# Routing rebuilt: the sample's tile first, each tile routed by itself behind the next tile's product

## The chip, the core and the metric

The kernel runs on one core of a Trainium2 chip. A core has a matrix engine (PE, with its weight loads PEld), three engines for elementwise work (DVE, ACT, POOL), and SP, which here issues DMAs. Each engine works through its own instructions in order, and semaphores order the engines against each other. The metric is the device time of one execution in microseconds.

## What is computed

One layer of a streaming encoder for 512 prompt tokens and 64 sample tokens of 1024 features, all in float32: adaLN modulation, one input projection, sparse attention beside a convolution branch, a gated merge, an output projection, a residual with LayerNorm, and a mixture of 16 experts in 4 groups. The part that matters here is the last one:

```python
x = layer_norm(ALPHA * x + (1 + gate_1) * (merged @ w_o))      # 512 + 64 rows
h = x * (1 + scale_2) + shift_2
gl = h @ w_group + b_group                  # 4 groups: the largest logit
rl = h @ w_router + b_router                # 4 x 4 experts: the two largest of the group
y = sum over the two experts of weight * (silu(h @ gate) * (h @ up)) @ down
x = layer_norm(ALPHA * x + (1 + gate_2) * y)
```

## The kernel before

Tokens lie in five tiles: t = 0..3 are the prompt's, 128 rows each, and t = 4 is the sample's, 64 rows. The **output projection** runs in two halves of 512 columns. In the first half five PSUM banks (`o0` to `o4`) are filled side by side. In the second half (`o1`, from two banks that are used in turn) the tiles follow each other: 24 matmuls for a prompt tile (three for each of 8 feature tiles, since values and weights are split into two parts, hi and lo), 16 for the sample's. After a tile's product DVE adds the residual (`residual`: `rt`, then `xn`), takes the row statistics (`bs`, `mv`), ACT the square root and the normalisation (`xn` in place), PE turns the normalised rows (`ph`, 8 transposes), ACT copies them (`h2T`), and PE multiplies them with the router's 20 columns (`prt`, 8 matmuls). `h2_rows` scales the rows and adds them to `h_scr` in DRAM, `ax_rows` does the same for the result's residual share (`z_scr`); of the five multiplications of `ax_rows`, DVE has two and POOL three.

**Routing** (`route`) runs in two batches, tiles 0 to 2 and tiles 3 and 4, when their logits are there: about 30 small DVE instructions a batch find the group, the two experts and their one-hot rows (`Ej`), PE counts the rows ahead of each (`prank`), DVE builds one-hot ranks (`ohr`), and PE turns them into lists of token numbers (`pid`). From these come `idt`, the rows that POOL gathers from `h_scr` for an expert (`xg`), and the weights (`pwt`, `wsl`). `table` writes slots and weights to DRAM with ten indirect DMAs (`ids_scr`), from which two small lists (`ido`, then `so`) are read back for second blocks of experts.

**Experts.** The first four are fixed, the others follow in the order of their number of rows. Unit by unit, weights come through a ring of 24 pieces, are split into hi (ACT) and lo (DVE), and PE multiplies: gathered rows turned (`pxt`), `pg` in four steps of six matmuls, `hm` (silu on ACT, product on DVE), turned again (`pht`, which in the program stands behind the next unit's first two steps), `pd`, and a scatter to `z_scr`. The list of PE, DVE and ACT from there on is written out by hand (`manual_schedule`). Up to there a scheduler orders the instructions of each engine. The weights of experts 0 to 2 and 3 are loaded ahead of it.

A few lines carry the steps (`G` is POOL, `V` DVE, `S` ACT):

```python
    (G if t > 1 else V).tensor_tensor(xn[t][0:n], xn[t][0:n], axr[0:n], op=OP.mult)
...
    route(0, 3)
    h2_rows(3)
    route(3, NT)
    h2_rows(4)
```

## Time and profile before

| | us |
|---|---|
| device time, median of 3 runs | 880.16 (871.29 to 882.45) |
| span of the profiled execution | 874.9 |
| PE busy | 786.5 (90%) |
| DVE busy | 637.2 (73%) |
| ACT busy | 357.5 (41%) |
| POOL busy | 148.5 (17%) |

The profiled execution lasted 874.9 us from its first to its last instruction; a time of its own is not given, and the median of the runs is 5.3 us above this span. Busy shares are means over the whole span. In the rows below, a row of the timeline is start, duration, engine, line, operation, output from input, shapes, how many instructions in a row are counted together, and in brackets how long the engine was idle before and what ended that.

### The profile page before, as it was taken

The page shows a single profiled execution, that of the slowest core. Times are in us where ns is not written, and L with a number is a line of the kernel's source. Part 1 is how long each engine was busy: PE and PEld are TensorE (multiplying, and loading weights), DVE is VectorE, ACT ScalarE, POOL GpSimd, SP SyncE. Part 2 cuts the span into 40 slices and gives each one's busy share as a digit, 9 for nine tenths or more (in the row PEclk, how much of TensorE's full clock was granted, in tenths as well). Part 3 has the DMA queues.
Part 4 walks back from the last instruction along what each step waited for, and adds up shares of the span by engine and source line. Part 5 has one row for each costly group of instructions (what it writes and reads, how often), then busy time and mean ns, then how long its engine had stood idle before and what let it go on. Part 6 is the DMA issues. An engine that isn't in the chain of part 4 may idle for free. (4 is left out here: it accounts for less than half of the span.)

```text
span 874.9 us, 13257 instructions
## 1 busy us (share of the span) xinstructions
PE 786.5 (90%) x4827; PEld 637.9 (73%) x4827; DVE 637.2 (73%) x1256; ACT 357.5 (41%) x647; POOL 148.5 (17%) x180
## 2 busy tenths in 40 slices
PE   4899999999999999999999999999946999999900
PEld 3788888887878879879899789988835676556200
DVE  1569999989999889988878434628795886674323
ACT  3243232324344335547743852322433664354213
POOL 2300000310100000000010001020348332322213
PEclk9999999999999999999999999999957999999965
DMA  9997664572523224232474205785897998799446
GB/s 291 341 350 248 210 199 128 116 252 56 148 73 93 80 75 115 89 100 65 133 204 130 61 1 184 244 273 193 174 309 203 335 367 290 204 359 348 113 121 110
DMA packets 109329, 161.53 MB, mean 185 GB/s; under 512 B 9730, under 2 KB 67226, under 8 KB 109264
## 3 DMA queue, kind: packets, MB, share of 16 engines
q1 hardware_dynamic: 93664, 117.49, 41.6%
q0 software_dynamic: 14000, 38.98, 17.9%
q10 hardware_dynamic: 1600, 4.22, 1.3%
q8 instruction: 38, 0.62, 0.3%
q14 instruction: 27, 0.22, 0.1%
HBM read 145.49 MB, written 28.49 MB: 199 GB/s over the span
## 5 line engine op out<-in xcount | busy, mean ns | idle before, releaser
L588 DVE SCALAR_TENSOR_TENSOR y<-ue,dwT,y 128x604 f32<-128x604 f32 (+17 forms) x232 | 183.5, 829 | 1.9 <-ACT y L586 1.5
L242 PE MATMUL acc<-hh,wlo 128*128 128x288 f32 (+1 forms) x504 | 152.8, 304 | 1.5 <-DVE wlo L140 1.5
L243 PE MATMUL acc<-hh,whi 128*128 128x288 f32 (+1 forms) x504 | 150.4, 299 | 0.0
L244 PE MATMUL acc<-hl,whi 128*128 128x288 f32 (+1 forms) x504 | 149.4, 300 | 0.0
L139 ACT CAST whi<-wraw 128x1024 fp32r<-128x1024 f32 (+1 forms) x72 | 75.0, 1043 | 170.7 <-PE acc L244 75.0
L140 DVE TENSOR_TENSOR wlo<-wraw,whi 128x1024 fp32r<-128x1024 f32 (+1 forms) x72 | 87.4, 1214 | 52.1 <-ACT whi L139 51.9
L242 PEld LDWEIGHTS acc<-hh,wlo 128*128 128x128 f32 (+1 forms) x504 | 94.2, 187 | 17.4 <-issue 8.8
L243 PEld LDWEIGHTS acc<-hh,whi 128*128 128x128 f32 (+1 forms) x504 | 94.3, 187 | 5.2 <-issue 5.1
L244 PEld LDWEIGHTS acc<-hl,whi 128*128 128x128 f32 (+1 forms) x504 | 93.7, 187 | 5.5 <-issue 5.2
L144 PE MATMUL tm<-wlo,hh 128*128 128x512 f32 x128 | 50.5, 397 | 0.4 <-DVE wlo L140 0.4
L145 PE MATMUL tm<-whi,hh 128*128 128x512 f32 x128 | 50.4, 394 | 0.0
L146 PE MATMUL tm<-whi,hl 128*128 128x512 f32 x128 | 49.8, 392 | 0.0
L140 DVE TENSOR_TENSOR wlo<-ring,whi 128x1024 fp32r<-128x1024 f32 x30 | 36.3, 1222 | 14.9 <-ACT whi L139 9.5
L1179 PE MATMUL pd<-ring,hT 128*128 128x512 f32 x96 | 43.7, 598 | 0.5 <-issue 0.5
L139 ACT CAST whi<-ring 128x1024 fp32r<-128x1024 f32 x30 | 31.3, 1050 | 28.6 <-PE pg L146 19.3
L242 PE MATMUL acc<-oh,wlo 128*128 128x288 f32 x128 | 39.1, 306 | 1.7 <-DVE gt L748 1.4
L244 PE MATMUL acc<-yl,whi 128*128 128x288 f32 x128 | 39.1, 308 | 0.6 <-DVE yl L725 0.5
L1194 POOL DMA_INDIRECT z_scr<-yo,idt x16 | 27.2, 1702 | 69.3 <-DVE yo L1190 19.4
L242 PE MATMUL acc<-yh,wlo 128*128 128x288 f32 x128 | 38.9, 305 | 0.0
L244 PE MATMUL acc<-ol,whi 128*128 128x288 f32 x128 | 38.1, 300 | 0.0
L243 PE MATMUL acc<-yh,whi 128*128 128x288 f32 x128 | 37.9, 298 | 0.0
L714 POOL DMA_DIRECT2D gates_scr<-glg x16 | 8.7, 542 | 171.9 <-ACT glg L713 93.1
(479 smaller groups left out, 1792.9 us busy)
## 6 DMA issues: line engine op xcount, KB each, us to landing
ring<-in_w_gate_up_dram SPq DMA_DIRECT2D x62, 512.0 KB
wraw<-in_w_in_dram SPq DMA_DIRECT2D x48, 512.0 KB
wada<-in_w_ada_dram SPq DMA_DIRECT2D x32, 512.0 KB
ring<-in_w_down_dram SPq DMA_DIRECT2D x32, 512.0 KB
wada<-in_w_ada_dram SPq DMA_DIRECT2D x32, 256.0 KB
gates_scr<-glg POOLq DMA_DIRECT2D x16, 288.0 KB
gt<-gates_scr POOLq DMA_DIRECT2D x16, 288.0 KB
wraw<-in_w_conv_out_dram SPq DMA_DIRECT2D x8, 512.0 KB
```

Of the source, the lines that this page charges most:

```text
L139: split_copy[0] = S.copy(hi, raw).ins
L140: V.tensor_tensor(lo, raw, hi, op=OP.subtract)
L144: PE.matmul(out, lh, rl, start=start, stop=False)
L145: PE.matmul(out, lh, rh, start=False, stop=False)
L146: PE.matmul(out, ll, rh, start=False, stop=stop)
L242: PE.matmul(ps[h][0:m, 0:288], wl[:, k, :], xh[:, k, sl], start=k == 0, stop=False)
L243: PE.matmul(ps[h][0:m, 0:288], wh[:, k, :], xh[:, k, sl], start=False, stop=False)
L244: return PE.matmul(ps[h][0:m, 0:288], wh[:, k, :], xl[:, k, sl], start=False, stop=k == KT - 1).ins
L588: V.scalar_tensor_tensor(y[:, 30 - i:EXT], ue[:, 0:EXT - 30 + i], dwT[:, j, i:i + 1], y[:, 30 - i:EXT], op0=OP.mult, op1=OP.add)
L714: G.dma_start(gates_d[m], sg)
L1179: PE.matmul(pd_[c], hT[:, k, :], dns[0][k][:, cs], start=k == 0, stop=k == 1)
L1194: sc = G.indirect_dma_start(out=z_d, out_offset=bass.IndirectOffsetOnAxis(ap=idx[0:128 // len(ids)], axis=0), in_=y[half], in_offset=None, ...
```

## The change

The order of the second half becomes `ORDER = [4, 0, 1, 2, 3]`. All of PE's, DVE's and ACT's instructions from there to the experts are now in the hand-written list. Behind each step of a tile's product stands one step of the tile before (`before`) : its residual and statistics, the turning, the router, the choice, the counts, the lists. The rows are turned and multiplied before they are normalised; the mean and the deviation are put right afterwards on the 24 logits (`swn`, `brs`). The router's eight matmuls stand in four strips of 32 columns of the array, and a ninth (`plog`) adds the strips. The choice uses DVE's instructions for the eight largest values and their places. POOL does no multiplication any more: DVE does all of `ax_rows`, the last two of them, the weights, the slots and `table` behind the second step of unit 0 (`behind_first`). Expert 2's weights are loaded ahead as before, expert 3's behind the gathered rows of block 0. ACT loads its tables for Exp and Silu in `weigh`, ahead of the gathered rows.

```diff
+ORDER = [4, 0, 1, 2, 3]
...
-    for t in range(NT):
+    for t in ORDER:
         residual(t, ps[t], 0)
+        half_stats(t, 0)
...
+        def turn(self, b):
+            t, n = self.t, self.n
+            if b == 0:
+                self.xT = wp.tile([128, KT, 128], F32, name="h2T", tag="wraw", bufs=2)
+            ph = trp("ph2")
+            for i in range(4):
+                k = 4 * b + i
+                PE.transpose(ph[:, 128 * i:128 * i + n], xn[t][0:n, 128 * k:128 * k + 128], ident[0:n, 0:n])
+            S.copy(self.xT[:, 4 * b:4 * b + 4, 0:n], ph.rearrange("p (k t) -> p k t", k=4)[:, :, 0:n])
+        def residual(self):
+            residual(self.t, self.po, 1)
+            half_stats(self.t, 1)
+            self.mean, self.rs = stats(None, self.n, bss[self.t])
+        def router(self, b):
+            n = self.n
+            if b == 0:
+                self.pr = dot("prt")
+            for j in range(4):
+                k = 4 * b + j
+                PE.matmul(self.pr[32 * j:32 * j + 32, 0:n], routers[self.s][:, k, :], self.xT[:, k, 0:n], start=b == 0, stop=b == 1,
+                          tile_position=(0, 32 * j))
+            if b == 1:
+                self.prs = late.tile([128, 128], F32, name="prs", tag="hm", bufs=3)
+                S.copy(self.prs[:, 0:n], self.pr[:, 0:n])
+        def logits(self):
+            n = self.n
+            self.pl = dot("plog")
+            PE.matmul(self.pl[0:n, 0:RE], self.prs[:, 0:n], strips[:, 0:RE], start=True, stop=True)
+        def normal(self):
+            n, t, x = self.n, self.t, xn[self.t]
+            if self.last:
+                h2 = self.h2 = h2s[self.p % 2]
+                V.scalar_tensor_tensor(h2[0:n], x[0:n], self.mean, GS[self.s][0:n], op0=OP.subtract, op1=OP.mult)
+                self.normed = S.activation(h2[0:n], h2[0:n], AF.Copy, scale=self.rs).ins
+                G.dma_start(dap(h2_d, t * 128 * D, [[D, n], [1, D]]), h2[0:n], accum_op=OP.add)
+                return
+            nm = late.tile([128, 1], F32, name="nm", tag="nm", bufs=2)
+            V.scalar_tensor_tensor(nm[0:n], self.mean, -1.0, self.rs, op0=OP.mult, op1=OP.mult)
+            S.activation(x[0:n], x[0:n], AF.Identity, bias=nm[0:n], scale=self.rs)
+        def h2_rows(self):
+            n, t = self.n, self.t
+            h2 = h2s[self.p % 2]
+            V.tensor_tensor(h2[0:n], xn[t][0:n], GS[self.s][0:n], op=OP.mult)
+            G.dma_start(dap(h2_d, t * 128 * D, [[D, n], [1, D]]), h2[0:n], accum_op=OP.add)
+        def ax_rows(self):
+            n, t, x = self.n, self.t, xn[self.t]
+            if self.last:
+                V.scalar_tensor_tensor(x[0:n], x[0:n], self.mean, axr[0:n], op0=OP.subtract, op1=OP.mult)
+                S.activation(x[0:n], x[0:n], AF.Copy, scale=self.rs)
+            else:
+                V.tensor_tensor(x[0:n], x[0:n], axr[0:n], op=OP.mult)
+            ax_sums.append(G.dma_start(dap(z_d, t * 128 * D, [[D, n], [1, D]]), x[0:n], accum_op=OP.add).ins)
+        def choose(self):
+            p, n, s = self.p, self.n, self.s
+            R = rlog[:, p, :]
+            V.scalar_tensor_tensor(R[0:n], swn[0:n, s, :], self.mean, self.pl[0:n, 0:RE], op0=OP.mult, op1=OP.add)
+            V.scalar_tensor_tensor(R[0:n], R[0:n], self.rs, brs[0:n, s, :], op0=OP.mult, op1=OP.add)
+            V.max(m8g[:, p, :], R[:, 0:RG])
+            V.max_index(i8g, m8g[:, p, :], R[:, 0:RG])
+            r16 = late.tile([128, 16], F32, name="r16", bufs=1)
+            V.tensor_tensor(r16, group16, i8g[:, 0:1].to_broadcast([128, 16]), op=OP.not_equal)
+            V.scalar_tensor_tensor(r16, r16, NEG, R[:, RG:RE], op0=OP.mult, op1=OP.add)
+            V.max(m8e[:, p, :], r16)
+            V.max_index(i8e[:, p, :], m8e[:, p, :], r16)
+            E = Ej[:, :, p, :]
+            V.tensor_tensor(E, iota16[:, None, :].to_broadcast([128, 2, 16]), bc(i8e[:, p, 0:2], 16), op=OP.is_equal)
+            V.tensor_tensor(mb[:, p, :], E[:, 0], E[:, 1], op=OP.add)
+            if s:
+                V.memset(mb[64:128, p, :], 0.0)
+        def places(self):
+            p = self.p
+            self.pk = dot("prank")
+            PE.matmul(self.pk[:, 0:16], tri, mb[:, p, :], start=True, stop=False)
+            PE.matmul(self.pk[:, 0:16], onesb, mp[:, p, :], start=False, stop=True)
+        def ranks(self):
+            p = self.p
+            if not ohr:
+                ohr.append(late.tile([128, 2, NT, 128], F32R, name="ohr", tag="ohr", bufs=1))
+            V.tensor_tensor(mp[:, p + 1, :], mp[:, p, :], mb[:, p, :], op=OP.add)
+            self.vid = late.tile([128, 2, 16], F32R, name="vid", tag="vid", bufs=2)
+            V.tensor_scalar(self.vid, Ej[:, :, p, :], tok1[:, p:p + 1], None, op0=OP.mult)
+            er = late.tile([128, 2, 16], F32, name="er", tag="er", bufs=1)
+            V.tensor_tensor(er, Ej[:, :, p, :], self.pk[:, None, 0:16].to_broadcast([128, 2, 16]), op=OP.mult)
+            V.tensor_reduce(rk[:, :, p], er, axis=AX.X, op=OP.add)
+            V.tensor_tensor(ohr[0][:, :, p, :], iota128[:, None, :].to_broadcast([128, 2, 128]), bc(rk[:, :, p], 128),
+                            op=OP.is_equal)
+        def tokens(self):
+            p, n = self.p, self.n
+            for j in range(2):
+                PE.matmul(pid[:, 0:16], ohr[0][0:n, j, p, :], self.vid[0:n, j, :], start=p == 0 and j == 0,
+                          stop=self.last and j == 1)
...
+    row, before, rowq = None, None, []
+    for p in range(NT):
+        before, row = row, Row(p)
+        rowq.append(row)
+        for k, _ in enumerate(row.product()):
+            if k == 0:
+                row.turn(0)
+                if before is not None:
+                    before.residual()
+            if k == 1:
+                row.router(0)
+            if before is None:
+                continue
+            if k == 2:
+                before.turn(1)
+                before.normal()
+            if k == 3:
+                before.router(1)
+                before.h2_rows()
+            if k == 4:
+                before.logits()
+                before.choose()
+            if k == 6:
+                before.places()
+                before.ranks()
+                if p < NT - 1:
+                    before.ax_rows()
+            if k == 7:
+                before.tokens()
+    row.residual()
+    row.turn(1)
+    row.normal()
+    row.router(1)
+    row.logits()
+    row.choose()
+    row.places()
+    row.ranks()
+    row.tokens()
...
+    def weigh():
+        V.tensor_tensor(gex, rlog[:, :, 0:4], bc(m8g[:, :, 0], 4), op=OP.subtract)
+        V.tensor_tensor(w12[:, :, 1], m8e[:, :, 1], m8e[:, :, 0], op=OP.subtract)
+        S.activation(gex, gex, AF.Exp)
+        S.activation(w12[:, :, 1], w12[:, :, 1], AF.Exp)
+        silu = late.tile([128, 1], F32, name="silu", bufs=1)
+        S.activation(silu, epst, AF.Silu)
...
+    with routing:
+        los = []
+        split_ahead(2, los)
+        weigh()
+        los.pop(0)()
+        with tc.issue_after(rows_in(0)):
+            load_first(3)
+        los.pop(0)()
+        split_ahead()
         pend, over = [], overflow()
+        def behind_first():
+            weights()
+            weight_columns()
+            room[True] = 1
+            slots()
+            for p in (NT - 2, NT - 1):
+                rowq[p].ax_rows()
+            gr0s.append(late.tile([128, D], F32, name="gr0", tag="row0", bufs=1))
+            brow(gr0s[0], rows_d, 4 * D)
+            table()
...
                 step(1, p, False)
+                if u == 0:
+                    behind_first()
```

Three places show what this does to the engines' lists. **PE, second half of the output projection.** Before, the second half begins with tile 0 (`o_6023`):

```order
L786 MATMUL pbr<-bw,ones 128x40
L144 MATMUL o_6023<-wo,mh 128x512
L145 MATMUL o_6023<-wo,mh 128x512
L146 MATMUL o_6023<-wo,ml 128x512
L144 MATMUL o_6023<-wo,mh 128x512
L145 MATMUL o_6023<-wo,mh 128x512
L146 MATMUL o_6023<-wo,ml 128x512
L144 MATMUL o_6023<-wlo,mh 128x512
```

Now it begins with the sample's (`o_6055`), and between the matmuls of the next tile (`o_6084`) stand the turning, the router, the logits, the counts and the lists of the sample's tile; here are the rows to the end of that tile's product:

```order
L157 MATMUL o_6084<-whi,mh 128x512
L158 MATMUL o_6084<-whi,ml 128x512
L1010 LDWEIGHTS tri
L1010 MATMUL prank<-mb,tri 128x16
L1011 LDWEIGHTS onesb
L1011 MATMUL prank<-mp,onesb 128x16
L156 MATMUL o_6084<-wlo,mh 128x512
L157 MATMUL o_6084<-whi,mh 128x512
L158 MATMUL o_6084<-whi,ml 128x512
L1029 MATMUL pid<-vid,ohr 128x16 x2
L156 MATMUL o_6176<-wo,mh 128x512
```

The logits (`plog`), the counts (`prank`) and the lists (`pid`) of one tile now stand ahead of the next tile's first matmul (`o_6176`) on PE. **DVE, between the two halves and in a tile.** Before, the first half's tile 0 comes first and the lists of the batches far behind:

```order
L800 TENSOR_TENSOR rt<-o_5821,rows_5791 128x512
L140 TENSOR_TENSOR wlo<-wraw,whi 128x1024
L789 TENSOR_TENSOR wrs<-wrt,gbT 128x160
L801 SCALAR_TENSOR_TENSOR xn_5810<-xn_5810,rt 128x512
L790 TENSOR_TENSOR wrt<-wrt,gbT 128x160
L800 TENSOR_TENSOR rt<-o_5822,rows_5791 128x512
L808 BN_STATS bs<-xn_5810 128x6
L801 SCALAR_TENSOR_TENSOR xn_5810<-xn_5810,rt 128x512
L788 TENSOR_TENSOR brs<-pbr,brt 128x40
L800 TENSOR_TENSOR rt<-o_5823,rows_5791 128x512
```

Now the first half's sample tile (`o_5846`) is first, and the residual of tile 0 (`o_5842`) stands behind it:

```order
L826 TENSOR_TENSOR rt<-o_5846,rows_5798 128x512
L809 TENSOR_TENSOR brs<-pbr,brt 128x48
L812 TENSOR_SCALAR swn<-pbr 128x48
L827 SCALAR_TENSOR_TENSOR xn_5826<-xn_5826,rt 64x512
L150 TENSOR_TENSOR wlo<-wraw,whi 128x1024
L829 TENSOR_TENSOR xn_5826<-xn_5826,rt 64x512
L834 BN_STATS bs<-xn_5826 64x6
L826 TENSOR_TENSOR rt<-o_5842,rows_5798 128x512
```

A tile's whole list then reads, for the first prompt tile (product `o_6084`):

```order
L986 TENSOR_TENSOR xn_5826<-xn_5826,axr 64x1024
L826 TENSOR_TENSOR rt<-o_6084,rows_5798 128x512
L827 SCALAR_TENSOR_TENSOR xn_5825<-xn_5825,rt 128x512
L834 BN_STATS bs<-xn_5825 128x6
L842 BN_AGGR mv<-bs 128x2
L844 RECIPROCAL mv<-mv 128x1
L970 SCALAR_TENSOR_TENSOR nm<-mv 128x1
L976 TENSOR_TENSOR h_6051<-xn_5825,rows_5798 128x1024
L992 SCALAR_TENSOR_TENSOR rlog<-swn,mv,plog 128x24
L993 SCALAR_TENSOR_TENSOR rlog<-rlog,mv,brs 128x24
L994 MAX m8g<-rlog 128x8
```

The normalised rows are scaled (`h`) ahead of the choice (`rlog`, `m8g`, ...), and the next tile's residual stands behind the whole of it. **DVE and POOL in unit 0.** Before, DVE had nothing but the splits and `hm` there, and POOL's ten scatters stood behind the three first gathers:

```order
L1116 DMA xg<-h_scr,idt 128x1024 x3
L1254 DMA ids_scr<-pay,slt 15552x2 x10
L1116 DMA xg<-h_scr,idt 128x1024
L1391 TENSOR_LOAD order
L1391 ISA x2
L1066 DMA cols<-cols 64x2x3
L1391 TENSOR_LOAD order
L1391 ISA x2
L1116 DMA xg<-h_scr,idt 128x1024
L1262 ISA
L1262 DMA ido<-ids_scr 128x2
```

Now, on POOL, they stand behind the last two rows of `z_scr`:

```order
L1225 DMA h_6051<-h_scr,idt 128x1024
L1176 DMA cols<-cols 64x2x3
L1225 DMA h_6050<-h_scr,idt 128x1024
L987 DMA z_scr<-xn_5825 128x1024
L770 DMA gr_6671<-rows_scr 128x1024
L987 DMA z_scr<-xn_5825 128x1024
L1360 DMA ids_scr<-pay,slt 15552x2 x10
L1225 DMA xg<-h_scr,idt 128x1024
L1304 DMA z_scr<-yo,idt 576x1024
L1368 ISA
L1368 DMA ido<-ids_scr 128x2
```

and DVE has, behind the copies of the weights and ahead of the splits that unit 1 needs (the `wlo` here is the first of them), the slots, the last two `ax_rows` and the table's payload:

```order
L1158 CAST sj<-i8e 128x5 x2
L1159 SCALAR_TENSOR_TENSOR sj<-sj,rk 128x10
L1160 CAST rki<-rk 128x10
L1161 TENSOR_SCALAR rki<-rki 128x10
L1162 CAST rk<-rki 128x10
L1164 SCALAR_TENSOR_TENSOR slt<-rk,sj 128x5 x2
L986 TENSOR_TENSOR xn_5825<-xn_5825,axr 128x1024
L983 SCALAR_TENSOR_TENSOR xn_5825<-xn_5825,mv,axr 128x1024
L1356 COPY pay<-w_6523 128x10
L150 TENSOR_TENSOR wlo<-ring,whi 128x1024
```

The lists that are read back (`ido`) are ten scatters, a scatter of rows and a gather later in this order than the sums of `z_scr`, and DVE's copies of them (`so`) stand in its list ahead of unit 2's splits.

## Rows read from the trace of the kernel before

**Rows 1.** Stretches: PE, PEld, DVE, ACT, POOL busy, granted clock, DMA share, GB/s.

```profile
630.00:640.00 10.00, 5.94 (x51) 5.64 (x51) 9.54 (x31) 4.74 (x7) 5.58 (x5) 0.72 1.07 260
640.00:650.00 10.00, 1.84 (x8) 1.51 (x8) 9.76 (x47) 3.37 (x5) 4.97 (x4) 0.50 1.04 293
```

**Rows 2.** Waits of PE from 590 to 730 us: total, times, longest.

```profile
PE pht L1161 <- DMA ids_scr<-pay,slt: 5.6, 1, 5.6
PE prank L944 <- DVE mb L940: 4.6, 1, 4.6
```

**Rows 3.** Timeline of PE: product, weights' columns, first expert matmul, turned hidden rows.

```profile
596.49 0.48 PE L144 MATMUL o<-wo,mh 128*128 128x512 f32 x1
...
628.14 0.40 PE L160 MATMUL o<-whi,ms 128*128 128x512 f32 x1
...
653.97 4.75 PE L1031 MATMUL pwt<-Ej,ohr 128*128 128x16 f32 x20 [0.69 <-DVE key L1045]
...
663.82 0.80 PE L144 MATMUL pg<-wlo,xhl 128*128 128x512 f32 x1
...
679.43 0.69 PE L1161 MATMUL pht<-ident,hm 128*128 128x128 f32 x2 [5.59 <-DMA ids_scr<-pay,slt]
...
690.88 0.38 PE L1161 MATMUL pht<-ident,hm 128*128 128x128 f32 x2
700.93 0.38 PE L1161 MATMUL pht<-ident,hm 128*128 128x128 f32 x2
```

**Rows 4.** Timeline of DVE: residual, statistics, scaling, small instructions, token numbers.

```profile
592.64 0.68 DVE L800 TENSOR_TENSOR rt<-o,rows 128x512 f32<-128x512 f32 x1
...
613.42 0.69 DVE L800 TENSOR_TENSOR rt<-o,rows 128x512 f32<-128x512 f32 x1
614.14 0.69 DVE L801 SCALAR_TENSOR_TENSOR xn<-xn,rt 128x512 f32<-128x512 f32 x1
...
617.83 1.22 DVE L891 TENSOR_TENSOR xn<-xn,axr 128x1024 f32<-128x1024 f32 x1
...
623.95 0.17 DVE L812 RECIPROCAL mv<-mv 128x1 f32<-128x1 f32 x1 [0.36 <-ACT mv L811]
...
638.25 0.17 DVE L913 SCALAR_TENSOR_TENSOR t<-t,iota 128x12 f32<-128x12 f32 x1
638.46 0.17 DVE L914 TENSOR_REDUCE ij<-t 128x3 f32<-128x12 f32 x1
...
651.41 0.69 DVE L953 TENSOR_TENSOR ohr<-iota,rk 128x512 fp32r<-128x512 f32 x1
...
653.52 0.16 DVE L1002 SCALAR_TENSOR_TENSOR idt<-pid,ise 128x4 int32<-128x4 f32 x1
```

**Rows 5.** Groups by line of DVE: the eight largest values; busy, mean ns.

```profile
L540 DVE MAX8 m<-sc 64x8 f32<-64x192 f32 x6 | 2.0, 340 | 0.0
```

**Rows 6.** Timeline of DVE beside a multiplication of POOL.

```profile
635.47 2.75 DVE L912 TENSOR_TENSOR t<-ing,m 128x12 f32<-128x12 f32 x1
```

**Rows 7.** Timeline of POOL: multiplication, first gather, first and last scatter, lists read back.

```profile
635.52 2.66 POOL L891 TENSOR_TENSOR xn<-xn,axr 128x1024 f32<-128x1024 f32 x1
...
655.78 3.22 POOL L1116 DMA_INDIRECT xg<-h_scr,idt  x1 [4.76 <-DVE wlo L140]
...
662.64 1.03 POOL L1254 DMA_INDIRECT ids_scr<-pay,slt  x1 [0.30 <-issue]
...
674.76 0.91 POOL L1254 DMA_INDIRECT ids_scr<-pay,slt  x1 [0.31 <-issue]
...
682.69 1.15 POOL L1262 DMA_DIRECT2D ido<-ids_scr  x2 [3.21 <-DMA ids_scr<-pay,slt]
```

**Rows 8.** Timeline of ACT: normalisation, table for Silu, first silu.

```profile
618.20 1.25 ACT L829 ACTIVATE xn<-xn,nm,mv 128x1024 f32<-128x1024 f32 x1
...
675.26 1.28 ACT L1154 ACT_TABLE_LOAD   x1
...
678.47 0.38 ACT L1154 ACTIVATE hm<-pg 128x256 f32<-128x256 f32 x1 [1.93 <-remote]
```

More of the change, by code (lines that the diff above doesn't have):

```diff
@@ L14 @@
 I32 = mybir.dt.int32
+U32 = mybir.dt.uint32
 AF = mybir.ActivationFunctionType
@@ new lines, in encoder_step @@
+    pbr = trp("pbr")
+    PE.matmul(pbr[:, 0:4 * NR], ones, bw.rearrange("p v s c -> p (v s c)"), start=True, stop=True)
+    brs = late.tile([128, 2, RE], F32, name="brs", bufs=1)
+    V.tensor_tensor(brs, pbr[:, 0:2 * NR].rearrange("p (s c) -> p s c", s=2)[:, :, 0:RE],
+                    brt[:, None, 0:RE].to_broadcast([128, 2, RE]), op=OP.add)
+    swn = late.tile([128, 2, RE], F32, name="swn", bufs=1)
+    V.tensor_scalar(swn, pbr[:, 2 * NR:4 * NR].rearrange("p (s c) -> p s c", s=2)[:, :, 0:RE], -1.0, None, op0=OP.mult)
@@ L793, in encoder_step @@
+    strips = late.tile([128, NR], F32, name="strips", bufs=1)
+    V.tensor_tensor(strips, ident[:, 0:NR], ident[:, NR:2 * NR], op=OP.add)
+    V.tensor_tensor(strips, strips, ident[:, 2 * NR:3 * NR], op=OP.add)
+    V.tensor_tensor(strips, strips, ident[:, 3 * NR:4 * NR], op=OP.add)
     xn03 = slot([128, 4, D], name="xn03")
@@ new lines, in token_kinds, with token_columns @@
+    def token_kinds(src, e0, e1):
+        V.tensor_scalar(sel[:, 1, e0:e1], src, float(SEQ), None, op0=OP.is_gt)
+        V.tensor_scalar(sel[:, 0, e0:e1], sel[:, 1, e0:e1], -1.0, 1.0, op0=OP.mult, op1=OP.add)
+    def token_columns(src, e0, e1):
+        token_ids(src, e0, e1)
+        token_kinds(src, e0, e1)
+    routed = token_ids(pid[:, 0:NFIX], 0, NFIX)
+    token_kinds(pid[:, 0:NFIX], 0, NFIX)
+    pids = late.tile([128, 2, NVAR], F32, name="pids", bufs=1)
+    V.tensor_copy(pids[:, 0, :], pid[:, NFIX:NE])
@@ new lines, in slots, with weight_columns @@
+            V.scalar_tensor_tensor(slt[:, :, j], rk[:, j, :], 2944.0, sj[:, j, :], op0=OP.mult, op1=OP.add)
+    def weight_columns():
+        pwt = fifth("pwt")
+        for j in range(2):
+            for p in range(NT):
+                n = TS[ORDER[p]]
+                PE.matmul(pwt[:, 0:16], ohr[0:n, j, p, :].bitcast(F32), Ej[0:n, j, p, :], start=p == 0 and j == 0,
+                          stop=p == NT - 1 and j == 1)
+        V.tensor_copy(wsl, pwt[:, 0:NFIX])
+        V.tensor_copy(pids[:, 1, :], pwt[:, NFIX:NE])
```

388 lines of the change are left out of this document (147 added, 241 removed).

## The prediction

> **What bounds the kernel now.** I read the stretches first, for the place where PE stands still: from 630 to 650 us PE is busy 5.9 and then 1.8 of 10 us, with a granted clock of 0.72 and 0.50, while DVE is busy 9.5 and 9.8 [rows 1]. So DVE, not PE, sets the end of the routing; the waits say the same, with 4.6 us of PE for the counts' input `mb` [rows 2]. Then the timeline of PE, for the marks that a walk can hold on to: the second half of the output projection runs from 596.5 to 628.5, the first expert matmul starts at 663.8, and the turned hidden rows of the first units (`pht`) come at 679.4, 690.9 and 700.9 [rows 3]. From there a unit takes 10.0 us and PE hardly waits, so whatever is late at the third `pht` is late at the end. The change touches nothing ahead of 590 us and nothing of the tail, so its whole worth is the shift of that mark. I walk along it with durations of the trace.
>
> **The start of the second half: +4.6 us.** Before, tile 0's product starts at 596.5 [rows 3] while DVE takes the first half's residuals from 592.6 on [rows 4]. In the changed order the first half's sample tile is DVE's first, and its product ends at 596.4, just ahead of the second half [rows 3]. The bank in which the second half is to begin is the one that tile 0's first half leaves, and that `rt` stands in DVE's list behind `rt`, two small operations, `xn`, a split of `wlo`, `xn` and `bs` of the sample. With 0.7 us for each 512-wide operation, 0.2 for the two small ones and 1.2 for the split (as for any two-input operation on 1024 values) [rows 4] that is 4 us, and 0.7 for the `rt` itself. The second half starts at about 601.1.
>
> **The tiles: product's end at about 650.8 instead of 628.5.** In a tile DVE must do, in this order: `ax_rows` of the tile before 1.2; `rt`, `xn`, `bs` 0.72 apart, 2.2; aggregate 0.2; the wait for ACT's root 0.4; reciprocal and `nm` 0.4 [rows 4]; the wait for ACT's normalisation, 1.25 [rows 8] and a hand-over, 1.4; the scaling `h` 1.2; the choice, ten operations that each need the one before; the counts on PE 0.3; the ranks, of which the last (256 wide) lies between 0.17 and the 0.69 us of 512 values, 1.2 [rows 4]. Two such dependent operations start 0.21 apart [rows 4], so the choice is 2.2 with a little for the two search instructions. Sum: 1.2+2.2+0.2+0.4+0.4+1.4+1.2+2.2+0.3+1.2 = 10.7 us. The trace has no such search over 8 or 16 values; bounds are the small operation's 0.17 [rows 4] and 0.34 for 192 values [rows 5], so four of them add 0 to 0.7 us a tile; I take the low end, because the width is nearer to it.
>
> PE's own work is less. The old second half holds 112 product matmuls, 40 transposes and most of the router in 32 us [rows 3], 6.8 us a tile; with the ninth router matmul, the counts and the lists I allow 7.9. But in each tile the next tile's `pid` and first matmul stand behind this tile's choice, so PE goes at DVE's 10.7. The first tile after the sample's pays the backlog of four first-half residuals on DVE, 2.1 us each, to about 609.9, and ends at 618.5; three more end at 618.5 + 3 x 10.7 = 650.6, with the last products behind it 650.8. The strips themselves cost PE next to nothing, since it waits there anyway.
>
> Against this stands one rule of the Trainium skill ("VectorE: DVE Perf Modes", "The TRN2 errata — SBUF-src ops pay a fixed extra latency per instruction"). This trace has 0.17 us for twelve values and 0.21 from one dependent start to the next [rows 4]. The table of that section gives VectorE 58 cycles plus one an element at 0.96 GHz, which by my estimate is 0.08 us for 16 values; the same section says that the table is too low. By the table some 16 small operations of a tile would be 1.5 us cheaper, and the total 6 us lower; the trace decides, I keep its 0.21, and 889 would lie inside the forecast's own band.
>
> **From the product's end to the token numbers: 10.9 us instead of 25.** Before, `idt` comes at 653.5 [rows 4], 25 us after the last product. Now only the last tile is left: its chain without `ax_rows` and with the two ACT steps, 10.9 us, so `idt` at 661.7. Net so far +8. In this the gain of the change is contained: the batches are gone, and with them the three multiplications of POOL, beside one of which a small DVE operation took 2.75 instead of 0.17 us [rows 6, 7]; all three together cannot have cost more than 3 x 2.66 = 8.0 us. That port is the mechanism in the Trainium skill too ("SBUF — State Buffer", "SBUF: two separate sides": DVE and GpSimd share ports, and the loser waits out the other's instruction), and the trace agrees, 2.75 beside 2.66.
>
> **To the first expert matmul: +4.3.** Before it was 10.3 us from `idt`, since POOL's first gather waited for a split on DVE and took 3.2 us [rows 7]. From that gather's start to the first `pg` it was 8.0 us [rows 3, 7]. Now POOL is free: the gather starts at 662.2, and if it takes 1.3 us, as the scatters are spaced, the first `pg` comes 6.0 us later, at about 668.1. Expert 3's load is out of the way there. It starts only behind these rows, but is needed some 45 us later; I cost it at nothing as long as the DMA share then stays under 1.
>
> **Unit 0: +5.** Before 15.6 us from the first `pg` to the first `pht`, 5.6 of them idle [rows 3]. Now DVE has two `xhl` and three splits, 5 us, and seven small operations, 1 us, ahead of the weighted one-hot rows, which are there at 674; PE's 20 `pwt` matmuls take till 676.8 (4.75 us at half clock before [rows 3], some 2.5 at full); DVE then does some twelve small operations (2.2) and two `ax_rows` (2.5) to 681.5; ACT normalises the last tile (1.25 [rows 8]) and splits (1.05), DVE the low part (1.2): unit 1's first matmul stands at about 684.8 and, twelve matmuls and a second split later, about 4 us, `pht` at 688.8: +9.4. If PE, DVE and ACT overlap better there, by the 5.6 us that PE had been idle before at the most, it is +4. Unit 1 then runs without the wait that made it 11.5 us long before: `pht` at 698.7, +7.8.
>
> **The lists that are read back: +7.** The ten scatters stand 12.1/9 = 1.3 us apart, and `ido` is read 7 us behind the last one [rows 7]. Now they begin behind the last `z_scr`, at 683.4; they end at 696.2, `ido` is issued at 703, and `so` can run at about 706. DVE's list has `so` ahead of unit 2's splits and would be there at 698.6, so DVE stands, and PE with it some 5 us after that: the third `pht` at 716 instead of 700.9, **+15**. This term has the widest bounds: with the scatters done 3 us earlier and landing in 3 instead of 7 us nothing waits (+8), with a slower landing it is +18.
>
> **Sum.** 874.9 + 15 = 890 for the span, and with the 5.3 us by which the median lies above it **895**.
>
> **Rivals.** (A) *The routing does hide.* If DVE's list keeps up, PE sets the pace of the tiles: 607.9 + 4 x 7.9 = 639.5 instead of 650.8, 11 us less, and with the lists' term still there +4; with it shortened −3. That gives 877 to 884, call it 880. For it: DVE is idle in the waits for ACT, where other work might fit; against it: the list is fixed, nothing may move into them. (B) *ACT's tables*, on the slower side. The Silu table load is 1.28 us in the trace, but the silu behind it starts 3.2 us after the load's start, the last 1.9 for nothing that is named [rows 8]. In the new list two table loads stand on ACT between expert 0's casts and the cast of the gathered rows. At 1.28 each they end before the rows land at 666.2; at 3.2 each the cast comes at about 671.6, and the first `pg` 4.5 us later: 895 + 4.5 = 900. It decides as soon as both together take over 4 us. (C) *The gain as a whole*: DVE is quick and the lists come in time, and the half clock after 640 us goes too. The first `pg` is then possible at 647: 17 us less than before, 863.
>
> **How the numbers follow.** Forecast 0.45 (895), A 0.20 (880), B 0.27 (900 to 906), C 0.08 (863 to 872). The 8 in 10 range takes in the bounds of the lists' term, B, and most of A: 878 to 906. A change of 2% (17.6 us) is about what a measurement of this kernel tells from none. Of the forecast's own band, some 0.32 lies under 897.8 and 0.13 above, B lies above, A is within, half of C is below 862.6: faster 0.05, same 0.55, slower 0.40.
>
> **What would show it.** Right: the first matmul of the second half at 601, PE's waits in it for `mb` and the bank, product's end near 651, `idt` 11 us later, `so` waiting for `ido` on DVE, and a steady 10.0 us a unit afterwards. Wrong: a product's end near 640 (the chain is shorter than its parts: A), an ACT gap behind the two table loads (B), or units longer than 10 us late on, which would mean that expert 3's delayed load reaches the ring after all.

## The result, and the profile after

The changed kernel takes 916.06 us (median of 4 runs, 913.12 to 917.83) against 878.67 us (871.29 to 882.45) for the kernel before: a ratio of 1.0437 [1.0385, 1.0489], slower. The forecast was 895 us with a range of 878 to 906, so the time lies outside it. The profiled execution took 917.83 us with a span of 916.2, 41.3 us longer than that of before.

I walk along the marks of the prediction, from the trace after (from the third `pht` on, the shift nearly stays: +41.3 in the span against +39.6 there):

| mark | before | forecast | after | shift forecast | shift measured |
|---|---|---|---|---|---|
| second half starts | 596.5 | 601.1 | 608.1 | +4.6 | +11.6 |
| last product | 628.5 | 650.8 | 660.2 | +22.3 | +31.6 |
| `idt` | 653.5 | 661.7 | 670.8 | +8.2 | +17.3 |
| first `pg` | 663.8 | 668.1 | 682.2 | +4.3 | +18.3 |
| first `pht` | 679.4 | 688.8 | 706.4 | +9.4 | +27.0 |
| second `pht` | 690.9 | 698.7 | 716.5 | +7.8 | +25.6 |
| third `pht` | 700.9 | 716.0 | 740.5 | +15 | +39.6 |

The timeline of PE after gives these marks; it answers to [rows 3].

```profile
600.81 0.39 PE L172 MATMUL o<-whi,ms 128*128 128x512 f32 x1
608.14 0.77 PE L169 MATMUL o<-wo,ms 128*128 128x512 f32 x1 [6.72 <-DVE rt L826]
...
638.01 0.17 PE L1010 MATMUL prank<-mb,tri 128*128 128x16 bf16 x1 [1.48 <-DVE mb L1003]
...
648.61 0.17 PE L1010 MATMUL prank<-mb,tri 128*128 128x16 bf16 x1 [1.48 <-DVE mb L1003]
...
659.79 0.39 PE L158 MATMUL o<-whi,ml 128*128 128x512 f32 x1
...
680.37 1.97 PE L1240 MATMUL pxt<-ident,h 128*128 128x128 f32 x8 [9.75 <-DMA h<-h_scr,idt]
682.16 0.79 PE L156 MATMUL pg<-wlo,xhl 128*128 128x512 f32 x1
...
688.42 4.63 PE L1171 MATMUL pwt<-Ej,ohr 64*128 64x16 f32 x20 [1.75 <-DVE Ej L1152]
...
706.44 0.38 PE L1271 MATMUL pht<-ident,hm 128*128 128x128 f32 x2
716.48 0.38 PE L1271 MATMUL pht<-ident,hm 128*128 128x128 f32 x2
...
734.14 0.76 PE L156 MATMUL pg<-wlo,xhl 128*128 128x512 f32 x1 [10.23 <-DVE wlo L150]
740.50 0.44 PE L1271 MATMUL pht<-ident,hm 128*128 128x128 f32 x2 [0.29 <-DVE hm L1265]
```

The reader is to see three long waits in brackets: 6.72 at the start, 9.75 for the gathered rows, 10.23 in the middle of unit 2. The distance of the tiles is 10.6 us (638.01 to 648.61). The stretches of after (columns as in [rows 1]) show where PE is idle: at the start, around the gather, and from 720 to 760.

```profile
600.00:610.00 10.00, 3.28 (x12) 1.85 (x10) 7.58 (x12) 1.04 (x1) 0.00 (x0) 0.83 0.94 336
...
640.00:650.00 10.00, 8.33 (x53) 5.27 (x52) 7.28 (x26) 2.76 (x5) 1.69 (x2) 1.00 0.59 93
660.00:670.00 10.00, 3.20 (x20) 1.87 (x19) 7.00 (x24) 5.25 (x7) 0.84 (x1) 0.57 1.01 323
670.00:680.00 10.00, 0.62 (x3) 0.53 (x3) 4.94 (x23) 1.80 (x4) 3.61 (x3) 0.50 0.83 241
...
720.00:760.00 40.00, 29.03 (x113) 19.99 (x112) 27.30 (x40) 16.30 (x23) 11.96 (x9) 0.83 1.01 344
```

DVE's timeline has the tile (scaling, search instructions) and the two ends of the later waits, `idt` and `so` (it answers to [rows 4, 5]).

```profile
634.48 1.23 DVE L976 TENSOR_TENSOR h<-xn,rows 128x1024 f32<-128x1024 f32 x1 [3.27 <-ACT xn L971]
...
645.08 1.22 DVE L976 TENSOR_TENSOR h<-xn,rows 128x1024 f32<-128x1024 f32 x1 [1.81 <-ACT xn L971]
...
646.77 0.17 DVE L994 MAX8 m8g<-rlog 128x8 f32<-128x8 f32 x1
646.97 0.09 DVE L995 MATCH_VALUE_LOAD i8g<-m8g,rlog 128x8 f32 x1
647.05 0.16 DVE L995 FIND_INDEX8 i8g<-m8g,rlog 128x8 uint32<-128x8 f32 x1
...
670.80 0.16 DVE L1083 SCALAR_TENSOR_TENSOR idt<-pid,ise 128x4 int32<-128x4 f32 x1
...
730.60 0.15 DVE L1370 CAST so<-ido 128x1 f32<-128x1 int32 x1 [14.09 <-DMA ido<-ids_scr]
```

POOL's timeline has the last rows' way to DRAM, the first gather, the first and last scatter and the read of the lists (it answers to [rows 7]).

```profile
665.82 0.84 POOL L967 DMA_DIRECT2D h_scr<-h  x1 [7.80 <-ACT prs L954]
675.40 1.56 POOL L1225 DMA_INDIRECT h<-h_scr,idt  x1 [8.74 <-DVE w L1138]
...
701.20 1.65 POOL L1360 DMA_INDIRECT ids_scr<-pay,slt  x1 [0.30 <-DVE wlo L150]
...
716.00 1.35 POOL L1360 DMA_INDIRECT ids_scr<-pay,slt  x1 [0.30 <-issue]
...
725.34 1.20 POOL L1368 DMA_DIRECT2D ido<-ids_scr  x2 [4.69 <-DMA ids_scr<-pay,slt]
```

The gather starts 4.6 us after `idt`. The profile names DVE's `w`, which ran shortly before POOL went on; experiment 4 shows that it isn't what POOL waited for.

**A part that isn't the change's.** The first half of the projection already ends 4.7 us late (601.2 instead of 596.5), in a stretch that the change doesn't touch. The groups of the two pages name the place: from 545 us on PE waits for `gt`, which stands on DVE behind the split of a weight load (the first row is of after, the second of before).

```profile
L254 PE MATMUL acc<-oh,wlo 128*128 128x288 f32 x128 | 40.1, 314 | 4.9 <-DVE gt L760 4.6
```

```profile
L242 PE MATMUL acc<-oh,wlo 128*128 128x288 f32 x128 | 39.1, 306 | 1.7 <-DVE gt L748 1.4
```

The wait explains 3.2 of the 4.7 us; behind it PE's granted clock from 540 to 560 us was 0.83, in before 1.00. Over the ten experiments the wait lies between 1.2 and 4.8 us, with no relation to the edit, and the first half ends between 596.1 us (experiment 3) and 602.7 (experiment 5). In experiment 7, whose instructions up to there are those of the kernel before, the wait is 4.7 and the half ends at 600.8, so this part is scatter between executions. A distance between two traces is therefore best counted from the end of the first half, the start of `pbr`: 596.35 in before and 601.04 in after. The end scatters too: the last 46 to 53 us of the span, behind the last wait for `hm`, differ by up to 7 us between the twelve traces. I compare experiments by distances inside a trace and take their medians with that grain.

### The profile page after: what moved, and what is told of

The parts are those of the page before. It is cut to its first block, busy times and chain, and to the rows that moved or that the text cites. A ratio compares the mean times of both kernels' runs of the same rounds, so it can differ in the third digit from the quotient of the medians.

```text
span 916.2 us, 13307 instructions
## 1 busy us (share of the span) xinstructions
PE 802.3 (88%) x4843; PEld 640.6 (70%) x4843; DVE 643.8 (70%) x1282; ACT 359.1 (39%) x654; POOL 139.9 (15%) x179
## 5 line engine op out<-in xcount | busy, mean ns | idle before, releaser
L156 PE MATMUL pg<-wlo,xhl 128*128 128x512 f32 x74 | 35.8, 484 | 11.8 <-DVE wlo L150 10.2
L150 DVE TENSOR_TENSOR wlo<-ring,whi 128x1024 fp32r<-128x1024 f32 x29 | 35.3, 1223 | 11.1 <-ACT whi L148 10.8
L255 PE MATMUL acc<-oh,whi 128*128 128x288 f32 x128 | 38.7, 303 | 0.0
```

Of the source, the lines that this page charges most:

```text
L150: V.tensor_tensor(lo, raw, hi, op=OP.subtract)
L156: PE.matmul(out, lh, rl, start=start, stop=False)
L255: PE.matmul(ps[h][0:m, 0:288], wh[:, k, :], xh[:, k, sl], start=False, stop=False)
```

## The experiments

All ten compute the whole layer. The ratios are to the kernel before as it ran beside them: a median of 875.83 us for the first four, 879.28 for 5 to 8, 877.3 for 9 and 10. The changed kernel itself ran only beside the result's, so differences from its 916.06 us are between groups of runs.

**1. The lists' consumers later.** DVE's three small operations `so` on a list move from the block's preparation to the start of unit 4.

```diff
-        V.tensor_copy(so[:, 0:1], ido[:, 0:1])
+        def kinds():
+            V.tensor_copy(so[:, 0:1], ido[:, 0:1])
...
+            if u == 4:
+                for kinds in late_kinds:
+                    kinds()
```

> The changed kernel with one edit: DVE's three small operations on each of the two lists that are read back (so from ido) stand at unit 4 instead of unit 2; the reads themselves stay. Theory L (DVE, in order, waits 14.1 us at so for ido, and PE stands for it 10.2 us): units 1 to 4 follow each other every 10 us, the gap between the second and the third pht falls from 24.0 to 10, and the time from 916 to 902 to 905. Rival W (expert 3's weights, whose second half is loaded only at about 705 us, are what unit 3 would wait for next): PE's wait moves to a split of the ring's pieces, the time falls by 5 us at most, to 911 or more.

904.23 us, ratio 1.0304 [1.022, 1.0387]. The timeline of PE shows the units at 10.0 us without a break; PE's wait of 10.2 us is gone.

```profile
701.99 0.38 PE L1271 MATMUL pht<-ident,hm 128*128 128x128 f32 x2
712.03 0.38 PE L1271 MATMUL pht<-ident,hm 128*128 128x128 f32 x2
722.05 0.38 PE L1271 MATMUL pht<-ident,hm 128*128 128x128 f32 x2
732.07 0.38 PE L1271 MATMUL pht<-ident,hm 128*128 128x128 f32 x2
```

The 14 us between the second and third `pht` of after (24.0 instead of 10.0) are the list that is read back, and nothing else (expert 3's weights are in time). The time is in the range that theory L gave.

**2. The first half's residuals in the order 0 to 4**, so that the bank of tile 0 comes free first.

```diff
-    for t in ORDER:
+    for t in range(NT):
         residual(t, ps[t], 0)
```

> The changed kernel with one edit: the first half's residuals in the order 0, 1, 2, 3, 4 again, so that tile 0's bank is free before the sample's first half is through. Theory S (the 6.7 us in which PE waits for rt ahead of the second half are on the path): the second half starts 4 to 6 us earlier and the time falls by as much, to 911. Rival B (DVE's backlog is the same in either order, and the sample's own residual, now last, holds the next step): the start is earlier, the product's end is not, 915 to 917.

918.71 us, 1.0479 [1.0399, 1.0559]. The second half starts at once, but the sample's residual is now DVE's last, and PE stands 9.6 us at the sample's transposes instead of 6.7 at the start. The wait has moved, not gone, as rival B had it: with the sample first, one of the two is always behind four residuals.

**3. The scaling `h` behind the choice.** `h2_rows` moves from step 3 of the product to the ranks.

```diff
                 before.router(1)
-                before.h2_rows()
...
                 before.ranks()
+                before.h2_rows()
```

> The changed kernel with one edit: in each of the four woven tiles the scaled rows h stand behind the choice and the ranks on DVE instead of ahead of them. Theory N (in each tile DVE stands 1.3 to 3.3 us for ACT's normalisation, and everything behind it with it): a tile takes 8.8 instead of 10.6 us, the product's end comes 6 to 8 us earlier, the time falls to 909. Rival P (PE's own work, 8.4 us of 10 in that stretch, and its waits in between hold the pace): a tile takes 10 us or more, 914 to 916.

909.31 us, 1.0375 [1.0283, 1.0467]. The tile is 10.83 us instead of 10.6. DVE no longer waits for ACT's normalisation, but for the logits, by 1.92 us: ACT copies the router's sums (`prs`) behind that normalisation. So theory N failed on the tile, although its time came about: in the profiled execution the span is 6.1 us shorter than in after, and 5.0 of these stand at the end of the first half already, ahead of the edit. Beside the edit, unit 0's `pwt` ran at a granted clock of 1.00 in this execution:

```profile
684.16 2.70 PE L1171 MATMUL pwt<-Ej,ohr 64*128 64x16 f32 x20 [1.57 <-DVE Ej L1152]
```

**4. Expert 2's weights behind the gathered rows**, where expert 3's already are.

```diff
-    load_first(2)
...
+            load_first(2)
             load_first(3)
```

> The changed kernel with one edit: expert 2's weights are loaded where expert 3's are, behind the gathered rows of block 0, instead of ahead of the gathers (there at 660 us, with a DMA share of 1.01 from 660 to 670). Theory G (POOL's first gather waits 4.6 us behind the token numbers for the landing of the last rows of h_scr, which share the DMA engines with that load): the gather starts 3 to 4 us earlier, and the time falls by 3 to 4, to 912. Rival F (the landing takes as long without the load, since it is a sum into DRAM of about 7 us in the kernel before): gather and time as they were, or, if expert 2's weights now come too late for unit 2, 5 to 10 us more.

905.86 us, 1.033 [1.0253, 1.0407]. In POOL's timeline the gather now starts 1.05 us after `idt` (667.92), with `w` still to come at 672.05:

```profile
662.93 0.84 POOL L967 DMA_DIRECT2D h_scr<-h  x1 [7.81 <-ACT prs L954]
668.97 1.12 POOL L1225 DMA_INDIRECT h<-h_scr,idt  x1 [5.19 <-DVE M L1109]
```

So in after POOL waits for the landing of the last tile's rows in `h_scr`, which share the DMA engines with expert 2's load (DMA share 1.01 from 660 to 670 us): the gather comes 9.6 us behind the write's issue there, 6.0 here. From the last `pid` to `pxt` it is 6.3 us instead of 10.4, the 4 us that theory G forecast. The median fell by 10, which the theory does not cover. In the profiled execution 2.6 of the rest lie between the start of the second half and the last product, where the two kernels' lists are the same, and 2.3 behind the third `pht`; that these belong to the edit is not shown.

**5. Tile 0 first, the sample's second** (with the token numbers' constants put right).

```diff
-ORDER = [4, 0, 1, 2, 3]
+ORDER = [0, 4, 1, 2, 3]
```

> The changed kernel with the order 0, 4, 1, 2, 3 instead of 4, 0, 1, 2, 3 (token numbers and payload follow it). Theory S (the sample's tile first is what makes the second half wait 6.5 to 8 us for DVE: its first half is the last to be through, and with only the residuals' order undone PE waited as long for its rows): PE goes on without a gap, the whole chain of tiles starts 6 to 8 us earlier, the time falls to 908 to 910. Rival B (the backlog of DVE is the same whichever tile is first): the gap moves into the first tile, 914 to 917.

907.61 us, 1.0308 [1.0242, 1.0373]. No gap is left at the start; three waits remain in the first tiles, 1.6 us for the turned rows and 0.9 and 1.4 for the residual. Counted from the end of the first half (602.73 us here), the span is 7.0 us shorter than in after, 4.3 of them at `idt`.

**6. The router's copy ahead of the normalisation on ACT**, and `h` behind the ranks as in 3.

```diff
             if k == 2:
                 before.turn(1)
-                before.normal()
             if k == 3:
                 before.router(1)
-                before.h2_rows()
+                before.normal()
...
                 before.ranks()
+                before.h2_rows()
```

> The changed kernel with two edits in the four woven tiles: the scaled rows h behind the ranks on DVE, as in the third experiment, and ACT's copy of the router's strips (prs) ahead of its normalisation instead of behind it. Theory C (with h behind the choice DVE waited 1.9 us for plog, since prs stands behind the normalisation on ACT; that loop and not PE holds a tile at 10.8 us): a tile takes 9.3 us, 1.3 us less than in the changed kernel, the token numbers come 5 us earlier, the time falls to 910. Rival P (PE's own 8.8 us of a tile with its waits): a tile stays above 10.3 us, the time at 914 to 916.

913.67 us, 1.038 [1.0315, 1.0445]. The tile is 10.54 us, as good as unchanged, as rival P had it. DVE waits 1.63 us for `plog`: from the finished residual the way is transposes, ACT's copy, router, ACT's copy, strips. `h` and `ax_rows` of one tile, 2.4 us, stand ahead of the next residual and so in the same loop.

**7. The kernel before, without POOL's multiplications.** The one part of the change that could have paid by itself.

```diff
-            (G if t > 1 else V).tensor_tensor(xn[t][0:n], xn[t][0:n], axr[0:n], op=OP.mult)
+            V.tensor_tensor(xn[t][0:n], xn[t][0:n], axr[0:n], op=OP.mult)
```

> The kernel before with one part of the change alone: DVE does the three multiplications of ax_rows that POOL did, and they end up behind the token numbers in its list. Theory M (DVE was blocked for some 7 us beside them): the token numbers come 6 to 7 us earlier, the first gather 3 to 6, and the time falls by 3 to 6 against the kernel before, to 872. Rival D (DVE is the bound, and the 3.6 us of multiplications that it now has, ahead of the splits and the gathered rows, give the rest back; the sums of z_scr land later and hold the scatters): within 2 us of the kernel before or up to 4 slower.

884.97 us, 1.0046 [1.0018, 1.0075], slower by a little. By the times of the traces the second `prank` is only 1.7 us earlier than before (648.60 instead of 650.32), but the first half ended 4.4 us later here, by the scatter that was named above. Counted from there, the second `prank` is 6.1 us earlier, `idt` 6.3 us (50.9 instead of 57.2 us behind) and the first gather 4.0. The first row is of before, the others of this run (`idt` of before is in [rows 4]):

```profile
596.35 0.31 PE L786 MATMUL pbr<-bw,ones 128*128 128x40 f32 x2
```

```profile
600.76 0.31 PE L786 MATMUL pbr<-bw,ones 128*128 128x40 f32 x2
...
651.63 0.16 DVE L1002 SCALAR_TENSOR_TENSOR idt<-pid,ise 128x4 int32<-128x4 f32 x1
```

So the first half of theory M holds, and the time is lost behind it, much as rival D had it: `z_scr`'s writes now stand behind the gathers. ACT waits there for a buffer that they free, and the casts of the gathered rows stand behind it:

```profile
677.19 1.04 ACT L139 CAST gs<-ring 128x1024 fp32r<-128x1024 f32 x1 [29.00 <-DMA z_scr<-xn]
678.14 1.07 ACT L1136 CAST xhl<-pxt 128x512 fp32r<-128x512 f32 x2
```

**8. Five edits together**: those of 1, 4, 5 and 6, and the slots and last two `ax_rows` moved ahead of block 0's gathered rows, into DVE's idle time.

```diff
         weigh()
         los.pop(0)()
+        slots()
+        for p in (NT - 2, NT - 1):
+            rowq[p].ax_rows()
```

> The changed kernel with five edits together: the lists' operations at unit 4 (first experiment), expert 2's load behind the rows (fourth), the order 0, 4, 1, 2, 3 (fifth), prs ahead and h behind (sixth), and the slots and the last two ax_rows ahead of the gathered rows of block 0, in the 6 us in which DVE waits for them, instead of in unit 0. If the terms add up (12 + 4 + 7 + 5 + 5 us), the time is 883. If the first edits only uncover the next wait, as DVE's backlog or the load of experts 2 and 3, 890 to 897.

891.87 us, 1.0147 [1.0085, 1.0209]: the best version, 24 us below after, still above the kernel before, in the range that was given for the case that the first edits uncover the next wait. Its `idt` comes at 663.18 and its first `pg` at 673.73, 10.6 us between them, about the 10.3 of before, and the units follow without a break (`pht` at 692.24, 702.25, 712.27). What it didn't reach of the sum is partly at the first `pg`: with the rows early, the moved `ax_rows` now stand in their way.

```profile
670.75 1.28 DVE L985 SCALAR_TENSOR_TENSOR xn<-xn,mv,axr 128x1024 f32<-128x1024 f32 x1
673.71 1.29 DVE L1248 TENSOR_TENSOR xhl<-pxt,xhl 128x512 fp32r<-128x512 f32 x2 [1.69 <-ACT xhl L1247]
```

**9. The tile filled**: with the copy ahead as in 6, `h` and `ax_rows` of a tile wait until the next tile's statistics are done, so that they fill DVE's wait for the logits.

```diff
-        before, row = row, Row(p)
+        older, before, row = before, row, Row(p)
...
             if k == 3:
                 before.router(1)
+                before.normal()
+                if older is not None:
+                    older.h2_rows()
+                    older.ax_rows()
```

> The changed kernel with the edits of the sixth experiment and one more: the scaled rows h and ax_rows of a tile stand on DVE behind the statistics of the next tile, in the 1.6 us in which DVE waits for the logits (plog), instead of ahead of the next tile's residual. Theory T (a tile's 10.5 us are a loop: residual, turning, copy, router, copy, plog, choice, ranks, and then h and ax_rows ahead of the next residual; DVE idles 2 of 10.5 us in it): without h and ax_rows in the loop a tile takes 8.8 to 9.2 us, the token numbers come 6 us earlier than in the changed kernel, and the time falls to 908 to 911. Rival P (PE's own 8.8 us with its own waits, or the last sums of h_scr landing later): a tile above 10 us, or the gather as late as before, 913 to 917.

911.0 us, 1.0382 [1.0326, 1.0438]. The tile falls to 9.85 us (631.62, 641.47, 651.31 for `prank`), not to the 8.8 to 9.2 expected, and DVE still waits 0.91 us for `plog`:

```profile
645.45 0.16 DVE L970 SCALAR_TENSOR_TENSOR nm<-mv 128x1 f32<-128x1 f32 x1
645.52 1.22 DVE L976 TENSOR_TENSOR h<-xn,rows 128x1024 f32<-128x1024 f32 x1
646.78 1.22 DVE L986 TENSOR_TENSOR xn<-xn,axr 128x1024 f32<-128x1024 f32 x1
648.91 0.24 DVE L992 SCALAR_TENSOR_TENSOR rlog<-swn,mv,plog 128x24 f32<-128x24 f32 x1 [0.91 <-PE plog L959]
```

The time is at the edge of the range that theory T gave, but the token numbers come only 2.9 us earlier than in after, counted from the end of the first half, and not 6. That gain is lost at once: the rows of the last two tiles are written to `h_scr` only at 657.9 and 658.4, beside expert 2's load, and PE waits 13.5 us for the gather, which starts 12.5 us behind the second of these writes.

**10. Seven edits**: 8 with the filled tile of 9, the weights' sums (`pwt`) right behind the first token numbers, and only the last `ax_rows` ahead of block 0.

```diff
     routed = token_ids(pid[:, 0:NFIX], 0, NFIX)
+    weigh()
...
     token_columns(cols[:, 0, 0:NFULL], NFIX, NFIX + NFULL)
+    weight_sums()
```

> The changed kernel with the edits of the eighth experiment, with two differences: h and ax_rows as in the ninth, the last tile's ax_rows alone ahead of the gathered rows; and one more, the weights (two Exp, their products and the 20 pwt matmuls) right behind the first token numbers, while PE waits for the gathered rows, instead of in unit 0. If the loop gives 6 us and unit 0 another 4 to 6: 880 to 883, level with the kernel before. If PE's wait for the gathered rows only grows by what unit 0 gives back: 887 to 890.

895.26 us, 1.0198 [1.0143, 1.0253], no better than 8 and above both ranges. The gather starts 5 us behind `idt` (669.57 and 664.55). As in 9 the rows of two tiles go to `h_scr` half a microsecond apart, and the gather comes 9.8 us behind the second write, here with no expert's load issued in between. Unit 2 has a new break, a weight load that comes late to the ring, as ACT's timeline shows:

```profile
711.99 1.04 ACT L149 CAST whi<-ring 128x1024 fp32r<-128x1024 f32 x1 [9.64 <-DMA ring<-in_w_gate_up_dram]
```

The loads that stand behind the gathered rows are issued from 674.56 us on here and from 669.23 in 8, while the second `pht` comes at 698.59 instead of 702.25: the ring has 9 us less. That this is the whole of the 9.64 is not shown, and a version with the weights early but without the filled tile wasn't run.

## Why the prediction was wrong

The direction of the shift and the mechanism of most of its terms came out, but the sum at the third `pht` was short by 24.6 us (39.6 measured, 15 forecast). Two steps failed by more than the scatter: the gather, taken to start as soon as the token numbers were there (5.0), and the lists that are read back (6.9). The start adds 2.3 and unit 0 3.6; some 7 us are scatter of the one profiled execution.

1. **"The change touches nothing ahead of 590 us"** is right, but the sum against one profiled execution was not safe by 4.7 us there: that much came from the wait for `gt` and the lower clock behind it. It is scatter and no part of the change: experiments 3 and 9, with the changed list, end the first half at 596.1 and 596.3 us, and experiment 7, with the list of before, at 600.8. The three runs that the prediction had of the kernel before spread from 871.29 to 882.45.
2. **The start, +4.6**: measured +6.9 (11.6 less 4.7). The mechanism is right, PE waits for DVE's `rt` behind the sample's operations. Missed, by my reading of the trace, was that the router's preparation on DVE (594.3 to 599.8 us, with a split among it) delays the last load of the projection's weights, so that their split on DVE waits for ACT until 604.74, with the `rt` behind it. Experiment 5 removes the whole gap.
3. **The tiles, 49.7 us from start to last product**: measured 52.0 in after, but 49.75 and 49.45 in experiments 1 and 4, whose lists are the same up to there. The term is right, and so is the tile of 10.7 (10.6 measured), and that DVE sets it, not PE; experiments 3, 6 and 9 show in addition that it's a loop through three engines (DVE, PE, ACT), which orders within it shorten by 0.75 us at best. The excess of 2.3 is again of the one execution. PE's product matmuls stand 0.43 us apart up to 616.8 us, behind the idle 6.7 us at the start, and again from 627.5 to 630.2 (granted clock 0.50 and 0.53, the 1.2 GHz level); elsewhere it is 0.23. In the first stretch DVE waits 1.48 us for PE, in the second its wait for ACT's normalisation is 3.27 us instead of the 1.81 of the next tile. Why the clock fell the second time, when PE's waits are much the same in every tile, stays open. So the first woven tile lasts 12.2 us from count to count (625.81 to 638.01), and 10.8 in experiments 1 and 4. PE is busy 8.3 of 10 us in the tiles, 8.8 a tile, so rival A's 7.9 was out of reach without DVE's chain too. The 0.21 us from one dependent small operation to the next held for the search instructions too (0.17 us, with 0.09 for the load of the values), at the low end, as taken. By the table of the Trainium skill ("VectorE: DVE Perf Modes", the section on the TRN2 errata) the choice would have been quicker; the trace after decides against the table, as the one before did. The same section has a second form, from measured additions, of N + 151 cycles at 0.96 GHz: by it 16 values would be 0.17 us (an estimate), and with that the 0.17 and 0.18 us of the trace agree.
4. **From the last product to `idt`, 10.9**: 10.6 measured. Right, with the gain of 14 us that the change makes here. The gain on POOL's side that this term held is real: experiment 7 has 6.3 us for it at `idt`, inside the forecast's bound of 8.0, so it would be close to half of the 14.
5. **From `idt` to the first `pg`, 6.4**: 11.4 measured, the clearest failed step. "Now POOL is free: the gather starts at 662.2", half a microsecond after `idt`, left out that the rows must have landed in `h_scr`; the gather starts 4.6 us after `idt` instead. I had costed expert 3's load and not expert 2's, which now starts at 659.99 and lands on the same engines. Experiment 4, without that load there, has the gather 1.05 us after `idt` and gives 4 us back; experiments 9 and 10 show that other writes just ahead of the last rows hold them as long. The remaining 0.8 us lie between the gather and the first `pg`.
6. **Unit 0, 20.7**: 24.3 measured. `pwt` took 4.63 us at a granted clock of 0.50 to 0.57 (the 1.2 GHz level most of the time), not 2.5. In experiment 3 it ran at 1.00 and took 2.70, and the same unit 0 took 22.0 us, so some 2.3 of the excess are the clock's. PE had waited as long for the gathered rows in that run (9.98 us, 9.75 in after), so that wait alone doesn't decide it; why the clock is back at the lower level for `pwt` in after stays open, and so does the other 1.3 us.
7. **The lists, +7**: +14.0 measured, the largest single term. The mechanism was the forecast's, `so` holds DVE and DVE holds PE's splits, and experiment 1 shows it. The size was off since the scatters started at 701.2, 17.8 us later than walked, while the second `pht` was 17.8 us later too, so the start alone cancels. What didn't cancel is their pace at a DMA share of 0.91 (0.74 in before), 16.2 us instead of 12.8 from the start of the first to the end of the last, and the way from that end to `so`, 13.3 us instead of 9.8 (the read issued 8.0 us behind it, not 6.8).

In numbers: 4.7 + 2.3 + 2.3 − 0.3 + 5.0 + 3.6 + 6.9 (from the first `pht` to the third, 34.1 us against 27.2) = 24.5, the rest is rounding. Of these the 4.7, the 2.3 of the tiles and some 2.3 of the 3.6 changed from one execution of the same list to another.

**The rivals.** A (880) and C (863) fell with the tile of 10.6 us. B fell too, though the time went its way: the table loads take 1.28 us each, the first runs at 667.59, and the silu stands right behind the second (675.11, then 676.40), so nothing is added. The forecast's fault was one of form as well: steps 5 and 7 were both taken from rows in which less stood beside them on the DMA engines, and each later mark hangs on the earlier ones, so their errors added where the range treated only one of them as wide.

**What stays.** In experiment 8, with the start, the gather and the lists put right, the span is 12.6 us longer than before, 2.0 of them at the end of the first half already. Counted from there, the last product comes 21.0 us later and the chain from it to `idt` is 13.3 us shorter, so `idt` is 7.7 us late; unit 0 adds 2.9, and the rest cancels. I put the 7.7 down to the weaving itself: batches let DVE do a small operation once for three tiles; woven, each of five tiles pays the chain, and PE, which waits about 1 us for `mb` in each, pays with it. No experiment isolates this.

## What to carry to other kernels

Weaving a serial chain into another engine's work cost the length of the chain here, since the engines work in order, and not only the work in it: walk the loop through all engines before counting on cover, and expect little from changing the order within it. A read of what has just been written to DRAM needs a place where nothing is queued behind its consumer; moved by two units here, it gave back 12 us by the medians. When loads move, check every one of them against the small transfers that someone waits for, not only the one that the change names. And before a mark of one trace is compared with that of another, count both from the last point that the change can't have moved: the size of experiment 7's gain hung on it.

## What the runs showed of the hardware

- DVE's eight largest values of 8 or 16 take 0.17 to 0.18 us and their places 0.16 to 0.17, with a separate load of 0.09; the group over 192 values before had 0.34 [rows 5].
- One small operation after another on DVE stood 0.21 us apart; beside POOL's multiplications one took 2.75 us, and with these on DVE `idt` came 6.3 us earlier (experiment 7).
- After the last 512 KB of rows were issued to be added into DRAM, the gather started 9.6 us later beside a weight load, 6.0 without one (experiment 4, where `idt` came only 1.05 us ahead of it), and 9.8 without one but with another tile's rows issued half a microsecond earlier (experiment 10).
- Ten indirect scatters of 128 rows stood 1.3 to 2.3 us apart at a DMA share of 0.91, 14.8 us from first to last issue, against 12.1 before at a share of 0.74 [rows 7].
- `pwt`'s 20 matmuls took 4.63 us at a granted clock of 0.50 to 0.57 and 2.70 at 1.00 (experiment 3).
- The output projection's first half ended between 596.1 and 602.7 us in the twelve traces, whatever the edit, with a wait behind an early load of 1.2 to 4.8 us in it.
